# How the norm factors of the attention's outputs and of the mixers reach all partitions: two small transfers through DRAM in place of a matmul with a diagonal

## The chip, the cores and the metric

The kernel runs on one core of one Trainium2 chip. The metric is the device time of one execution in microseconds (us). Below, PE is the matmul engine, DVE the vector engine, ACT the scalar engine, POOL the GpSimd engine and SP the engine from whose queue most transfers are started; a transfer can also be started from POOL or ACT. Each engine works through its own instructions strictly in the order in which they stand. An instruction that has to wait therefore holds up everything behind it on its engine. SBUF is the on-chip memory with 128 partitions, PSUM the banks that PE writes.

## The reference

One step of a one-layer hybrid decoder. A prompt of 1024 tokens with 16 meta tokens ahead of it and 8 running sequences with 4 new tokens each go through the same layer, 1072 tokens in all. In float32:

```
u   = rmsnorm(h, norm1_g) @ w_in            # q, k, v, z, xbc, dt
ao  = sliding-window attention (window 128, sinks)          # 512 wide
y   = ssd_scan(conv(xbc), dt, ...) + xs * d_skip
so  = rmsnorm(y * silu(z), ssm_out_g)                       # 512 wide
h   = h + concat(rmsnorm(ao, attn_out_g), so) @ w_out
h   = h + relu(rmsnorm(h, norm2_g) @ w_up)**2 @ w_down
out = rmsnorm(h, norm_f_g)
```

The change touches two of these norms: that of the attention's outputs `ao` and that of the mixers' outputs `y * silu(z)`. Each needs, per token, the factor (mean of squares + 1e-6) to the power -1/2 over 512 values.

## The kernel before, in words

Activations lie transposed: features on the partitions, tokens along the free axis. The tokens are cut into 9 tiles: tile 0 holds the 32 sample tokens and the 16 meta tokens, tiles 1 to 8 hold 128 prompt tokens each. Three neighbouring tiles make a chunk, and the large matmuls work chunk by chunk (three chunks of about 384 tokens).

A float32 matmul is emulated for the projections: a matrix is split into a high and a low part of a faster float32 format, and three products are added. Such a group is 24 matmuls (12 for half the depth). Five stages follow each other: input projections with the attention of the tiles between them (to about 299 us), the output projection with the mixers of the tiles (the SSD scan, to about 411 us), the second half of the output projection with the second norm, the up projection, and the down projection with the last norm.

In the first two stages the work around the change is written as Python generators. `interleave` takes a stream of matmul groups and a list of chains with starting slots: in each slot every live chain is advanced to its next `yield`, and then the stream issues its next group. So a `yield` in a chain means "one matmul group later". `attn_block(i)` of tile i starts in the slot `START[i]`, 3.3 slots after its neighbour; `mixer(i)` starts 2.25 slots after its neighbour. This program order is a wish, not yet the order on the engines: the framework that builds the program gives each instruction its place in its engine's row by the priority that the program order gives it and by when it expects the operands to be there. So it can move an instruction ahead of others, and does.

A tile's norm goes like this. `norm_o(i)` (attention) or `gate(i)` (mixer) lets ACT square the 4x128 values of each token (`sqo`, `sqy`). `rms_bcast` then adds the four blocks, on POOL for the attention (line 369 and 370) and on DVE for the mixers, and PE multiplies them with a column of ones, so that the sum of squares of token p stands on partition p, one number per partition. `rstd_of` turns it into the factor `rsb`: one DVE instruction (line 322) and a power on POOL (line 323). The factor is needed the other way round, though: on every partition, along the free axis. ACT scales the identity matrix by the factor, which gives a diagonal matrix `dg` (line 378), and PE multiplies a matrix of ones with it. All 128 partitions of a PSUM bank (tag `pt` in the attention, `s` in the mixers) then hold the factors of the 128 tokens. DVE multiplies the tile by that bank: line 773 (`qT<-qT,pt`) in the attention, four instructions of line 1192 (`xs<-xs,vec,s`) in a mixer. From these results ACT and DVE or POOL make the split operands (`acth`, `actl`) of the output projection, and the first projection that reads them comes a stage or several groups later.

`late_of(i)` lets the attention's broadcast wait for a slot in which no other chain wants a `pt` bank.

Of the kernel before, what the change touches and what calls it, by code (L numbers as in the profile page):

```python
# [9 lines left out]
F32 = mybir.dt.float32  # L10
# [10 lines left out]
NT = 9  # L21
# [167 lines left out]
def f(ap):  # L189
    return ap.bitcast(F32)  # L190
# [3 lines left out]
def body(ctx: ExitStack, tc: tile.TileContext, xT, xm, win, wdt, wo, wu, wd, ck, cv, sc, st, sT, vec, consts,  # L194
         y, kp, vp, cv_, hp, ko, kn, vo, vn, hsm):
    nc = tc.nc
    PE, ACT, DVE, POOL, SP = nc.tensor, nc.scalar, nc.vector, nc.gpsimd, nc.sync
    vec_in, sc_in, st_in, sT_in = vec, sc, st, sT

    def pool(name, bufs=1, **kw):  # L200
        return tc.tile_pool(name=name, bufs=bufs, reuse_waits="tile", **kw)

    def mm(out, a, b, start, stop, on=False):
        PE.matmul(out, lhsT=a, rhs=b, start=start, stop=stop, skip_group_check=on)  # L204
# [3 lines left out]
    dram = ctx.enter_context(pool("dram", space=bass.MemoryType.DRAM))  # L208
# [40 lines left out]
    class Ahead:  # L249
# [9 lines left out]
        def next(self):  # L259
            while self.fns and len(self.got) <= self.n:  # L260
                self.more()
            return self.got.pop(0)
# [56 lines left out]
    def rstd_of(out, ssq, n):  # L319

        w = out.shape[-1]
        DVE.tensor_scalar(out=out, in0=ssq, scalar1=1.0 / n, scalar2=EPS, op0=ALU.mult, op1=ALU.add)
        POOL.tensor_tensor(out=out, in0=out, in1=nhalf[:out.shape[0], :w], op=ALU.pow)  # L323
# [11 lines left out]
    def act_cols(X, i):  # L335

        ch = i // 3
        a, w = TOKM[i][0] - CM[ch][0], TOKM[i][1]
        return X[ch][0][1][:, :, a:a + w], X[ch][1][1][:, :, a:a + w]
# [20 lines left out]
    pa = w2.enter_context(pool("pa"))  # L360
# [3 lines left out]
    def ps_tile(tag):  # L364
        return pps.tile([128, 512], F32, name=tag, tag=tag, bufs=1 if tag == "o" else 2)

    def rms_bcast(wk, eng, bank, sq, rows, n, *tags, late=0):

        eng.tensor_tensor(out=sq[:, 0:2], in0=sq[:, 0:2], in1=sq[:, 2:4], op=ALU.add)
        eng.tensor_tensor(out=sq[:, 0], in0=sq[:, 0], in1=sq[:, 1], op=ALU.add)  # L370
        yield
        yield
        ps = bank(*tags[:1])
        mm(ps[:rows, 256:257], sq[:, 0], ones[:, 0:1], True, True)
        rs = wk.tile([128, 1], F32, name="rsb", tag="rsb", bufs=2)
        rstd_of(rs[:rows], ps[:rows, 256:257], n)
        dg = wk.tile([128, 128], F32, name="dg", tag="dg", bufs=2)
        ACT.activation(out=dg[:rows, :rows], in_=ident[:rows, :rows], func=AF.Copy, scale=rs[:rows])
        for _ in range((2 if eng is DVE else 1) + late):
            yield  # L380
        ps = bank(*tags[1:])
        mm(ps[:, :rows], ones[:rows, :], dg[:rows, :rows], True, True)
        return ps
# [313 lines left out]
    def attn_block(i):  # L697
# [56 lines left out]
        o = po[:, :4 * rows].rearrange("p (r t) -> p r t", r=4)  # L754
        ACT.copy(out=qT[:, :, q0:q0 + rows], in_=o)
        yield from norm_o(i, o)

    START = [0] + [24 + round(3.3 * (i - 1)) for i in range(1, NT)]

    def late_of(i):  # L760

        if i == 0 or i == NT - 1:
            return 0
        taken = {START[n] + q for n in range(1, NT) for q in (3, 4)}
        return next(n for n in range(9) if START[i] + 8 + n not in taken)

    def norm_o(i, o_ps=None):
        r0, rows = TOK[i][0], TOKM[i][1]
        o = qT[:, :, r0:r0 + rows]
        sq = pa.tile([128, 4, 128], F32, name="sqo", tag="sqo", bufs=1)  # L770
        ACT.activation(out=sq[:, :, :rows], in_=o if o_ps is None else o_ps[:, :, :rows], func=AF.Square)
        ps = yield from rms_bcast(pa, POOL, ps_tile, sq[:, :, :rows], rows, 512, "o", "pt", late=late_of(i))
        DVE.tensor_tensor(out=o, in0=o, in1=ps[:, :rows].unsqueeze(1).broadcast_to([128, 4, rows]), op=ALU.mult)

    def attn_sample():
# [87 lines left out]
    def first():  # L863
        yield from attn_sample()
        kS.append(pa.tile([128, 2, 2, 2, 128], F32R, name="kS", tag="kS"))
        split_k(0)
        yield
        yield from norm_o(0)
# [44 lines left out]
    sq = {}  # L913
    w3 = ExitStack()
    sp = w3.enter_context(pool("sp"))
# [38 lines left out]
    for a, b in ((xs0, xs), (bc0, bc)):  # L954
        POOL.tensor_copy(out=a[:, :, 0:32].rearrange("p j (b t) -> p j b t", t=4),
                         in_=b[:, :, 0:56].rearrange("p j (b t) -> p j b t", t=7)[:, :, :, 0:4])
# [75 lines left out]
    def xcols(i):  # L1032
        if i == 0:
            return xs0, bc0[:, 0:2], bc0[:, 2:4]
        a = conv_col(TOK[i][0])
        return xs[:, :, a:a + 128], bc[:, 0:2, a:a + 128], bc[:, 2:4, a:a + 128]
# [4 lines left out]
    def ssd(i):  # L1041
# [70 lines left out]
        else:  # L1112
# [8 lines left out]
            for j in range(4):  # L1121
                yield
                if j == 3:
                    yield
                yield from sample_state(j, xw, Bt, eA)
        yield from gate(i)

    Bm = [None]
# [51 lines left out]
    def gate(i):  # L1180

        r0, rows = TOK[i][0], TOKM[i][1]
        y = xcols(i)[0][:, :, :rows]
        zt = sp.tile([128, 4, 128], F32, name="zt", tag="zt", bufs=2)
        SP.dma_start(out=zt[:, :, :rows], in_=zd[:, :, r0:r0 + rows])
        DVE.scalar_tensor_tensor(out=y, in0=y, scalar=0.5, in1=zt[:, :, :rows], op0=ALU.mult, op1=ALU.mult)
        sq = sp.tile([128, 4, 128], F32, name="sqy", tag="sqy", bufs=1)
        ACT.activation(out=sq[:, :, :rows], in_=y, func=AF.Square)
        yield
        ps = yield from rms_bcast(sp, DVE, ptile, sq[:, :, :rows], rows, 512)  # L1190
        for j in range(4):
            DVE.scalar_tensor_tensor(out=y[:, j], in0=y[:, j], scalar=vec[:, V_GS + j:V_GS + j + 1], in1=ps[:, :rows],
                                     op0=ALU.mult, op1=ALU.mult)
        hi, lo = act_cols(X, i)
        ACT.copy(out=hi, in_=y)
        POOL.tensor_tensor(out=lo, in0=y, in1=f(hi), op=ALU.subtract)
# [28 lines left out]
    rb = pu.tile([128, TM], F32, name="rb")  # L1225
# [6 lines left out]
    def bank(tag):  # L1232
        return pp5.tile([128, 512], F32, name=tag, tag=tag, bufs=3 if tag == "b" else 2) if tag != "g" else gps()
# [490 lines left out]
    for i, (j, k) in enumerate(down):  # L1724
# [19 lines left out]
        if j == 3 and 6 <= k < 6 + 2 * NE:  # L1744
            n, x = (k - 6) // 2, (k - 6) % 2
# [70 lines left out]
    for i, (c, k, ms) in enumerate(last):  # L1816
# [6 lines left out]
        if k == 0:  # L1823
            ps = {3: ps3} if c and ms == (3,) else {m: bank(t) for m, t in zip(ms, "ccgg" if c == 0 else "bbg")}
# [42 lines left out]
```

## Time and profile before

| | before |
|---|---|
| time, median of 3 runs | 1129.27 us (1129.19 to 1129.62) |
| the profiled execution | span 1128.1 us from the first to the last instruction; the page gives no other time of it |
| PE, share of the span busy | 98% |
| DVE | 74% |
| ACT | 50% |
| POOL | 20% |
| granted PE clock | 0.998 |

The 1128.1 us are the stretch between the first and the last instruction of one execution; the 1129.27 us are the whole of an undisturbed one, 1.2 us more. In the views below a row of a timeline reads: start in us from the span's start, length in us, engine, line of the kernel, operation, tile written, an arrow, tiles read, and in square brackets how long the engine had been idle before it and which instruction ended that. Consecutive matmuls overlap, so the time one costs is the distance from its start to the start of the next. A group of rows is written with its count, and "fp32" matmuls of the plain kind appear as two records each.

### The profile page before, as it was taken

To read this page: it belongs to the slowest core of one execution; us is meant where nothing else is said; L and a number is where in the kernel's file an instruction comes from. 1 tells how busy PE (TensorE), PEld (TensorE's weight loads), DVE (VectorE), ACT (ScalarE), POOL (GpSimd) and SP (SyncE) were. 2 spreads that over 40 slices of the span, in tenths; PEclk is the share of its full clock that TensorE was granted. 3 is DMA by queue.
4 is the path that set the end of the run, shared out by engine and by line. 5 is a ranking of instruction groups with operands and counts; after the bars stand their busy time and mean duration, and the time that the engine had idled before them with its cause. 6 is when DMAs were issued, how large, how long until landed. Compare 5 with 4: busy or idle time off the path is not lost.

```text
span 1128.1 us, 21791 instructions
## 1 busy us (share of the span) xinstructions
PE 1110.9 (98%) x8403; PEld 1072.7 (95%) x8403; DVE 838.3 (74%) x1624; ACT 569.6 (50%) x1205; POOL 223.5 (20%) x291
## 2 busy tenths in 40 slices
PE   8999999999999999999999999999999999999997
PEld 8989988889888899999999999999999999999997
DVE  6646888985788968998877777766599656867483
ACT  8312467575675748854444444444434334546361
POOL 0442365664344441210000000000000000000001
PEclk9999999999999999999999999999999999999999
DMA  8131100111466476666653443524999654465273
GB/s 287 70 98 38 38 24 34 38 53 42 144 211 196 142 268 219 211 191 216 211 190 106 162 153 134 178 90 170 384 307 322 191 172 109 118 197 169 76 229 111
DMA packets 84424, 177.64 MB, mean 157 GB/s; under 512 B 10692, under 2 KB 32740, under 8 KB 82272
## 3 DMA queue, kind: packets, MB, share of 16 engines
q1 hardware_dynamic: 77392, 141.59, 40.2%
q0 software_dynamic: 6224, 33.74, 7.5%
q8 instruction: 66, 1.08, 0.4%
q10 hardware_dynamic: 704, 0.92, 0.2%
q14 instruction: 38, 0.31, 0.1%
HBM read 125.49 MB, written 50.72 MB: 156 GB/s over the span
## 4 chain that ended last, share of the span: by engine, by line
PE 77%; DVE 10%; ACT 5%; issue 3%; DMA 3%; POOL 1%; POOLq 0%; SPq 0%; ACTq 0%; DVEq 0%
PE g L204 42%; PE b L204 19%; PE c L204 9%; PE s L204 3%; PE o L204 1%; ACT p L681 1%; DMA wraw<-in_win 1%; DVE Qs L712 1%; PE y L204 1%; DMA wdr<-in_wd 1%; DMA wraw<-in_wo 1%; DVE Sd L1612 1%; PE pt L745 1%; DVE p L679 1%; DVE bc L526 1%
## 5 line engine op out<-in xcount | busy, mean ns | idle before, releaser
L204 PE MATMUL g<-acth,whi 128*128 128x384 f32 (+2 forms) x528 | 161.9, 331 | 0.2 <-DVE qT L456 0.2
L204 PE MATMUL g<-acth,wlo 128*128 128x384 f32 (+2 forms) x528 | 159.3, 327 | 1.2 <-DVE hb L996 1.2
L204 PE MATMUL g<-actl,whi 128*128 128x384 f32 (+2 forms) x432 | 140.6, 325 | 0.0
L1625 ACT CAST ts<-tr 128x528 fp32r<-128x528 f32 x92 | 58.2, 632 | 119.2 <-PE b L204 99.2
L1626 DVE TENSOR_TENSOR ts<-tr,ts 128x528 fp32r<-128x528 f32 x92 | 64.9, 705 | 54.5 <-ACT ts L1625 53.8
L204 PEld LDWEIGHTS g<-acth,whi 128*128 128x128 f32 x528 | 97.3, 188 | 2.1 <-issue 1.0
L204 PEld LDWEIGHTS g<-acth,wlo 128*128 128x128 f32 x528 | 97.1, 188 | 1.5 <-DVE hb L996 1.3
L204 PEld LDWEIGHTS g<-actl,whi 128*128 128x128 f32 x432 | 81.4, 189 | 0.1
L323 POOL TENSOR_TENSOR rs<-rs,nhalf 128x3 f32<-128x3 f32 x9 | 10.4, 1153 | 334.5 <-DMA wdq<-in_wd 285.5
L1341 ACT COPY s<-g 128x264 f32<-128x264 f32 x90 | 33.9, 377 | 62.0 <-PE g L204 61.5
L236 POOL TENSOR_TENSOR wlo<-wraw,whi 128x256 fp32r<-128x256 f32 x56 | 50.0, 924 | 11.8 <-ACT whi L233 11.6
L1414 POOL DMA_DIRECT2D u<-u x16 | 8.5, 533 | 177.0 <-ACT u L1357 147.2
L1346 DVE TENSOR_TENSOR u<-b,s 128x264 f32<-128x264 f32 x64 | 27.4, 429 | 19.5 <-PE b L204 10.1
L735 POOL TENSOR_TENSOR p<-p,sm 128x512 f32<-128x512 f32 (+1 forms) x32 | 34.3, 1093 | 31.4 <-DVE sm L733 29.6
L1351 ACT ACTIVATE u<-u 128x528 f32<-128x528 f32 x42 | 27.1, 646 | 26.4 <-DVE u L1350 26.4
L204 PE MATMUL b<-ts,w7y 128*128 128x264 f32 x279 | 39.3, 285 | 0.0
L204 PE MATMUL g<-ts,whi 128*128 128x264 f32 x279 | 38.9, 284 | 0.0
L204 PE MATMUL g<-ts,w7y 128*128 128x264 f32 x279 | 38.9, 283 | 0.0
L204 PE MATMUL b<-ts,whi 128*128 128x264 f32 x279 | 38.9, 284 | 0.0
L204 PE MATMUL g<-ts,wlo 128*128 128x264 f32 x270 | 38.0, 285 | 0.0
L204 PE MATMUL b<-ts,wlo 128*128 128x264 f32 x270 | 37.3, 282 | 0.0
L681 ACT ACTIVATE p<-p,nm 128x257 f32<-128x257 f32 (+1 forms) x64 | 31.3, 492 | 11.0 <-DVE nm L679 10.8
(584 smaller groups left out, 3475.7 us busy)
## 6 DMA issues: line engine op xcount, KB each, us to landing
tr<-u SPq DMA_DIRECT2D x92, 264.0 KB, 3.1
wraw<-in_wu SPq DMA_DIRECT2D x38, 512.0 KB, 4.0
wdr<-in_wd SPq DMA_DIRECT2D x68, 256.0 KB, 4.0
u<-t POOLq DMA_DIRECT2D x16, 1056.0 KB, 5.6
wraw<-in_win SPq DMA_DIRECT2D x16, 512.0 KB, 3.7
u<-u POOLq DMA_DIRECT2D x10, 792.0 KB, 3.6
wraw<-in_wo SPq DMA_DIRECT2D x24, 256.0 KB, 2.9
h<-he SPq DMA_DIRECT2D x16, 264.0 KB, 5.2
```

The source lines that it names most:

```text
L204: PE.matmul(out, lhsT=a, rhs=b, start=start, stop=stop, skip_group_check=on)
L236: eng.tensor_tensor(out=lo[:, n], in0=raw[:, n], in1=f(hi[:, n]), op=ALU.subtract)
L526: DVE.scalar_tensor_tensor(out=acc, in0=cb[:, j:j + CL], scalar=cw_(j), in1=acc, op0=ALU.mult, op1=ALU.add)
L679: DVE.tensor_tensor_reduce(out=s_out[:, 0:W], in0=ps, in1=mask, scale=-scale, scalar=nsink, op0=ALU.add, op1=ALU.min, accum_out=nm)
L681: ACT.activation(out=s_out[:, 0:W + 1], in_=s_out[:, 0:W + 1], func=AF.Exp, bias=nm, scale=-1.0, accum_out=sm)
L712: DVE.tensor_tensor(out=Q[oth, g, :, :rows], in0=src, in1=f(Q[own, g, :, :rows]), op=ALU.subtract)
L735: POOL.tensor_tensor(out=p[:rows, r:r + 2, :W], in0=p[:rows, r:r + 2, :W], in1=sm[:rows, r:r + 2].unsqueeze(2).broadcast_to([rows, 2, W]), ...
L1341: ACT.copy(out=s[:, c], in_=ps[c][:, :TQ])
L1346: DVE.tensor_tensor(out=out[:, c], in0=ps[c][:, :TQ], in1=s[:, c], op=ALU.add)
L1351: ACT.activation(out=x, in_=x, func=AF.Square)
L1625: ACT.copy(out=t[:, 0], in_=x)
L1626: DVE.tensor_tensor(out=t[:, 1], in0=x, in1=f(t[:, 0]), op=ALU.subtract)
```

## The change

In the first eight tiles of each of the two norms the diagonal matrix and the matmul with it go. The column of factors `rsb` is written by a transfer from POOL's queue into a small DRAM tensor (128 numbers of 4 bytes). One slot later a transfer in SP's queue reads that tensor back as a row of 128 numbers and writes it to every partition, into an SBUF tile `rbc` of 128x128 numbers. One slot after that (and `late` more) the tile is multiplied by `rbc` as before by the PSUM bank. The last tile, number 8, of each norm keeps the old way. The tile `rbc` takes its place from the same two buffers as `dg` had.

```diff
+    rsd = {}
+
-    def rms_bcast(wk, eng, bank, sq, rows, n, *tags, late=0):
+    def rms_bcast(wk, eng, bank, sq, rows, n, *tags, late=0, key=None):
...
         rstd_of(rs[:rows], ps[:rows, 256:257], n)
+        if key:
+            rd = rsd[key] = dram.tile([128, 1], F32, name=f"rd{key}")
+            POOL.dma_start(out=rd[:rows], in_=rs[:rows])
+            yield
+            rb = wk.tile([128, 128], F32, name="rbc", tag="dg", bufs=2)
+            SP.dma_start(out=rb[:, :rows], in_=rd[:rows].rearrange("p q -> q p").broadcast_to([128, rows]))
+            for _ in range(1 + late):
+                yield
+            return rb
         dg = wk.tile([128, 128], F32, name="dg", tag="dg", bufs=2)
         ACT.activation(out=dg[:rows, :rows], in_=ident[:rows, :rows], func=AF.Copy, scale=rs[:rows])
         for _ in range((2 if eng is DVE else 1) + late):
             yield
...
-        ps = yield from rms_bcast(pa, POOL, ps_tile, sq[:, :, :rows], rows, 512, "o", "pt", late=late_of(i))
+        ps = yield from rms_bcast(pa, POOL, ps_tile, sq[:, :, :rows], rows, 512, "o", "pt", late=late_of(i), key=f"o{i}" if i < NT - 1 else None)
...
-        ps = yield from rms_bcast(sp, DVE, ptile, sq[:, :, :rows], rows, 512)
+        ps = yield from rms_bcast(sp, DVE, ptile, sq[:, :, :rows], rows, 512, key=f"y{i}" if i < NT - 1 else None)
```

PE loses 16 matmuls and ACT 16 instructions; POOL gains 16 transfers and SP 16. In the first stage the order of PE is otherwise the same. In the mixers' stage the framework also puts other instructions of all engines into a slightly different order.

Three places show what moves. The first is DVE in the attention of tile 3, eleven rows behind the one that starts the factor (`rsb`, line 322). Before, the multiply of `qT` by the bank `pt` stands behind the scaling of the next projection (`cb<-g,rb`):

```order
L694 TENSOR_TENSOR kS<-kT,kS 64x128
L695 TENSOR_TENSOR kS<-kT,kS 64x128
L733 RECIPROCAL sm<-sm 128x4
L447 TENSOR_TENSOR cb<-g,rb_133 128x384
L773 TENSOR_TENSOR qT<-qT,pt 128x4x128
L526 SCALAR_TENSOR_TENSOR bc<-cb,vec,bc 128x1096
```

With the change (its line numbers are up to 11 higher):

```order
L705 TENSOR_TENSOR kS<-kT,kS 64x128
L706 TENSOR_TENSOR kS<-kT,kS 64x128
L744 RECIPROCAL sm<-sm 128x4
L784 TENSOR_TENSOR qT<-qT,rbc 128x4x128
L458 TENSOR_TENSOR cb<-g,rb_133 128x384
L537 SCALAR_TENSOR_TENSOR bc<-cb,vec,bc 128x1096
```

The multiply stands one place earlier, ahead of `cb`, though the program order has it a slot later. In tile 4 the same happens, and in tiles 2 and 6 it moves ahead of more rows; in tiles 1, 5 and 7 its place is unchanged.

The second place is SP in the attention of tiles 1 to 5. Before, one load of weights (`wraw`) stands behind the other:

```order
L630 DMA out_kp<-kT 128x128
L631 DMA out_vp<-vt 128x128
L231 DMA wraw<-in_win 128x1024 x9
L897 DMA out_cv_<-tail 128x216
L231 DMA wraw<-in_win 128x1024
L668 DMA zd<-thz 128x304
```

With the change (`rdo` is the DRAM tensor of one tile):

```order
L231 DMA wraw<-in_win 128x1024 x2
L384 DMA rbc<-rdo_1743 128x128
L231 DMA wraw<-in_win 128x1024
L384 DMA rbc<-rdo_1939 128x128
L231 DMA wraw<-in_win 128x1024
L384 DMA rbc<-rdo_2203 128x128
L231 DMA wraw<-in_win 128x1024
L384 DMA rbc<-rdo_2413 128x128
L908 DMA out_cv_<-tail 128x216
```

A read of factors stands between every two loads of weights; each waits there until its write has landed.

The third place is DVE at the end of the mixers, with tiles 7 and 8. Before (each group of `xs<-xs,vec,s` belongs to the `rsb` above it):

```order
L1192 SCALAR_TENSOR_TENSOR xs<-xs,vec,s 128x128 x4
L322 TENSOR_SCALAR rsb<-s 128x1
L246 TENSOR_TENSOR wlo<-wraw,wlo 128x512
L971 TENSOR_TENSOR hb<-hb,g 128x288
L1192 SCALAR_TENSOR_TENSOR xs<-xs,vec,s 128x128 x2
L971 TENSOR_TENSOR hb<-hb,g 128x384
L1192 SCALAR_TENSOR_TENSOR xs<-xs,vec,s 128x128 x2
```

With the change:

```order
L322 TENSOR_SCALAR rsb<-s 128x1
L246 TENSOR_TENSOR wlo<-wraw,wlo 128x512
L982 TENSOR_TENSOR hb<-hb,g 128x288
L1203 SCALAR_TENSOR_TENSOR xs<-xs,vec,s 128x128
L1203 SCALAR_TENSOR_TENSOR xs<-xs,vec,rbc 128x128 x4
L1203 SCALAR_TENSOR_TENSOR xs<-xs,vec,s 128x128
L982 TENSOR_TENSOR hb<-hb,g 128x384
L1203 SCALAR_TENSOR_TENSOR xs<-xs,vec,s 128x128 x2
```

Tile 7's four multiplies, which stood ahead of the `rsb` of tile 8, now stand behind it, between the multiplies of tile 8.

## The prediction

> **What bounds the kernel now.** I read the page first, then the busy times of the two stages that the change touches (rows: stretch, length, busy us of each engine with its number of instructions, granted clock, DMA share and GB/s).
>
> ```profile
> span 1128.1 us, 21791 instructions
> PE 1110.9 (98%) x8403; PEld 1072.7 (95%) x8403; DVE 838.3 (74%) x1624; ACT 569.6 (50%) x1205; POOL 223.5 (20%) x291
> ...
> 125.00:300.00 175.00, 172.22 (x1108) 157.82 (x1107) 138.33 (x311) 107.26 (x277) 95.83 (x124) 1.00 0.14 41
> 300.00:330.00 30.00, 28.38 (x223) 23.83 (x222) 26.59 (x53) 22.07 (x59) 10.89 (x11) 1.00 0.76 229
> 330.00:411.00 81.00, 79.32 (x586) 70.43 (x585) 69.39 (x161) 49.49 (x123) 36.96 (x37) 1.00 0.57 175
> ```
>
> PE is busy nearly all the time in both stages, at full clock, so a matmul taken away should be worth its time. But DVE has 138.33 of 175 us and 69.39 of 81 us of work, so PE is not far ahead of it. The list of what PE waited for says where it already is not alone:
>
> ```profile
> PE pt L745 <- POOL p L735: 1.7, 4, 0.6
> ```
>
> Four times PE waited for the softmax rows that POOL scales. The chain of waits (start, length, what), followed back from the end, shows what set those moments:
>
> ```profile
> 172.16 4.18 PE g L204 x24
> 176.34 0.02 issue
> 176.36 0.49 DVE cb L447
> ...
> 211.40 0.94 ACT whi L233
> 212.34 1.22 ACT bc L524
> ...
> 230.29 0.39 POOL p L735
> ...
> 241.95 0.88 PE pt L745 x6
> ...
> 344.48 0.69 DVE hn L1099
> ...
> 354.27 1.12 DVE xs L1192 x4
> ...
> 364.23 0.29 ACT dg L378
> ...
> 367.06 0.49 PE s L204 x2
> ```
>
> From 176.36 to 241.95 us, the attention of tiles 2 to 4, the chain runs over DVE, ACT and POOL, and not over PE. From 344.48 us to the multiply at 354.27 and on to ACT at 364.23 it again does not pass PE. Elsewhere in the two stages it is PE's.
>
> **What goes from PE.** Each broadcast is two records; I take the distance from its start to the next other matmul. First and last of the seven attention tiles that go (1 to 7; tile 0 is alike), then first and last of the eight in the mixers:
>
> ```profile
> 168.76 0.38 PE L204 MATMUL pt<-dg,ones 128*128 128x128 f32 x2
> 169.08 1.51 PE L204 MATMUL o<-pT,vt 128*64 128x512 f32 x6
> ...
> 285.79 0.38 PE L204 MATMUL pt<-dg,ones 128*128 128x128 f32 x2
> 286.10 1.94 PE L204 MATMUL o<-pT,vt 128*64 128x512 f32 x8
> ...
> 340.17 0.49 PE L204 MATMUL s<-dg,ones 128*128 128x128 f32 x2
> 340.59 1.09 PE L204 MATMUL y<-Mt,xd 128*64 128x128 f32 x14
> ...
> 406.12 0.38 PE L204 MATMUL s<-dg,ones 128*128 128x128 f32 x2
> 406.34 0.28 PE L204 MATMUL s<-ones,sqy 128*128 128x1 f32 x2
> ```
>
> Attention: 8 x 0.32 = 2.57 us (tile 0 has 0.33). Mixers: 0.42 where small matmuls follow and 0.22 where large ones do; three of the first kind, three of about the second (0.24 once) and two that stand together at 0.66 make 2.60. In all 5.17 us.
>
> Not all of it is on the path. The broadcasts of attention tiles 2, 3 and 4 lie in the stretch that DVE and ACT set: 3 x 0.32 = 0.96 us only lengthen PE's waits. The same holds for the second mixer's 0.42, at 349.7 us. That leaves 5.17 - 1.38 = 3.79. ACT's own instruction (`dg`) is on the chain once, 0.29 us at 364.23; the other 15 lie beside waits of ACT. Gain: **4.08 us**.
>
> **What comes in its place.** The factor now travels: power on POOL, start of the write on POOL, landing, SP sees it and starts the read, landing, multiply on DVE. No such pair is in the trace. The nearest rows (line, queue, count, KB, median us from start to landing; the last one is POOL's time for starting a transfer):
>
> ```profile
> s1d<-s POOLq DMA_DIRECT2D x6, 264.0 KB, 3.2
> zt<-zd SPq DMA_DIRECT2D x1, 64.0 KB, 2.4
> out_kn<-kT SPq DMA_DIRECT2D x1, 16.0 KB, 1.4
> dtw<-in_wdt SPq DMA_DIRECT2D x1, 32.0 KB, 3.8
> L1368 POOL DMA_DIRECT2D s1d<-s x6 | 3.3, 542 | 12.3 <-ACT s L1341 12.3
> ```
>
> Lower bound of the pair: twice the smallest store, 2.8 us. Upper bound: the store from POOL's queue and the slowest small load, 3.2 + 3.8 = 7.0. For the write I take the middle of 1.4 (its size, another queue) and 3.2 (its queue, far larger), 2.3; for the read of 64 KB the row of that size, 2.4. Estimate: **4.7 us** from the end of the power to `rbc`.
>
> [...]
>
> Tile 3 of the attention decides the first stage, for there DVE and ACT set the time:
>
> ```profile
> 206.89 0.55 POOL L323 TENSOR_TENSOR rsb<-rsb,nhalf 128x1 f32<-128x1 f32 x1 [2.55 <-DVE rsb L322]
> 208.88 0.10 POOL L641 MEMSET cb<- 128x3 f32 x1 [1.45 <-DVE bc L533]
> ...
> 211.44 0.18 DVE L733 RECIPROCAL sm<-sm 128x4 f32<-128x4 f32 x1 [0.50 <-ACT p L681]
> 211.53 0.53 DVE L447 TENSOR_TENSOR cb<-g,rb 128x384 f32<-128x384 f32 x1
> ```
>
> The power ends at 207.44 us and the multiply is due behind the reciprocal at 211.6, so the pair has 4.2 us: DVE waits 4.7 - 4.2 = 0.5. Behind the multiply now stands `cb`, and ACT's `bc` reads that. `cb` ended at 212.06 and ACT, behind its `whi`, started `bc` at 212.34 (the chain above), 0.3 us later; now `cb` ends later by the multiply (0.68) and the wait, so ACT starts 0.4 + 0.5 = **0.9 us** later. That is on the chain. In tile 4 the same happens, but there the chain leaves DVE with POOL's row at 230.29, which depends on the reciprocal ahead of the multiply: nothing counted. Tile 2, moved the same way but with the factor long there: 0.1.
>
> POOL's start of the write, 0.54 us, falls into the 1.45 us for which POOL waits at 208.88; uncovered, 16 of them would cost 8.7 us. SP stands still at each read until the write has landed. Behind it in the first stage is a load of weights that waits longer anyway; in the mixers it is the loads and stores of `hb`, which three buffers keep ahead of DVE.
>
> Tile 5 has the tightest place, and tile 7 the tightest of the mixers:
>
> ```profile
> 245.08 0.55 POOL L323 TENSOR_TENSOR rsb<-rsb,nhalf 128x1 f32<-128x1 f32 x1 [3.19 <-DVE rsb L322]
> 247.02 0.57 DVE L447 TENSOR_TENSOR g<-g,rb 128x384 f32<-128x384 f32 x1 [0.96 <-PE g L204]
> 247.50 0.68 DVE L773 TENSOR_TENSOR qT<-qT,pt 128x512 f32<-128x512 f32 x1
> 249.89 0.48 DVE L679 CUSTOM_DVE_ANT_0 p<-s,cmk,vec 128x256 f32<-128x256 f32 x1 [1.02 <-PE s L204]
> ...
> 404.21 0.66 POOL L323 TENSOR_TENSOR rsb<-rsb,nhalf 128x1 f32<-128x1 f32 x1 [0.31 <-DVE rsb L322]
> 410.67 0.61 DVE L1192 SCALAR_TENSOR_TENSOR xs<-xs,vec,s 128x128 f32<-128x128 f32 x2 [1.73 <-PE s L204]
> ```
>
> Tile 5: power done at 245.63, multiply due at 247.50, 1.9 us, so DVE waits 2.8. Queued behind it is the scores' reduction (`p`, line 679), for which ACT, POOL and then PE wait. DVE had 0.96 + 1.02 us of idle here, and PE writes three `g` banks ahead; I count 0.2 for tiles 5 to 7. Mixer 7: power done at 404.87, so `rbc` at 409.6, and DVE gets there at 410.67 or later; but a large load stands ahead of this read in SP's queue. With mixer 0, whose multiply is also near, 0.4 for the mixers.
>
> **The sum.** 4.08 - (0.9 + 0.1 + 0.2 + 0.4) = 2.48 us gained. Against the profiled execution: span 1128.1 - 2.5 = 1125.6. The median of the runs lies 1.2 above that span, so I predict 1129.27 - 2.48 = **1126.8 us**. Its own range goes from all losses away (1125.2) to losses twice as large (1128.4).
>
> **Rivals.** (1) *The DVE row pays for the whole.* The pair takes longer than 4.7 us, and DVE, which cannot pass the multiply, holds the chain. With a pair of P, tiles 3 and 4 lose 0.4 + (P - 4.2) each, tile 5 half of what exceeds its 1.9 + 2.0 us, and mixers 0.4 to 1.2. At P = 5.3 that is 3.0 + 0.7 + 0.4 = 4.1, the whole gain; at 6.4 it is 5.2 + 1.3 + 1.1 = 7.6, so 3.5 us slower: 1132.8. For it: small loads of 3.8 us, DVE at 79% and 86%. Against it: the transfers are idle 86% of the first stage (share 0.14), and tile 4 may hide its part. [...]
>
> (2) *The new order of the mixers eats their gain.* The framework reordered that stage, and PE is idle there for only (30.00 - 28.38) + (81.00 - 79.32) = 3.3 us, so any reorder can cost. If the mixers' 2.60 us are lost, 0.1 us slower than before: 1129.4. For it: DVE is the fuller engine there. Against it: the order was made with eight matmuls fewer, and nothing long was put ahead of the scan.
>
> (3) *Everything counts.* DVE does not wait and the stretch of tiles 2 to 4 is PE's after all, since PE waits only 1.7 us there: 5.17 us, 1124.1.
>
> (4) *The change does not do what it says*: 16 matmuls stay. The order of PE shows them gone; 1129.3.
>
> **Chances and range.** Forecast 0.46, (1) 0.18, (2) 0.18, (3) 0.16, (4) 0.02. What one measurement can tell from no change is 0.2%, 2.26 us, so faster means below 1127.0. Two thirds of the forecast's range lie there: 0.31 + 0.16 = 0.47 faster. Same: 0.15 of the forecast, 0.14 of (2), (4): 0.31. Slower: (1) and 0.04 of (2): 0.22. Range for 8 in 10: from 1124.0, rival (3), to 1131.5, where (1) stands at P = 6.0.
>
> **What would show it.** Right: `pt<-dg` and `s<-dg` only once each; `rbc` landing 4 to 5.5 us after the power; DVE waiting for `rbc` about 0.5 us at tiles 3 and 4 and 2 to 3 us at tile 5; PE still busy for 98% and its waits for line 735 longer by 1 to 2 us. Wrong: a pair above 5.3 us; waits of PE for DVE in the attention of over 3 us together; in the mixers, PE idle more than 4 us longer; or a first stage that ends later than 299 us.

## The result and the profile after

The changed kernel takes **1241.74 us** (median of 4 runs, 1236.28 to 1245.51), the kernel before 1129.23 us beside it: a ratio of 1.0989, interval 1.096 to 1.1017. The prediction was 1126.8 us, in a range from 1124.0 to 1131.5. The change costs 112.5 us where a gain of 2.5 was forecast.

First the page of the changed kernel (its span, the busy time of each engine, and the granted clock in 40 slices of 31 us), then the busy times of three stretches of it in the columns of the prediction's second view:

```profile
span 1239.0 us, 21783 instructions
PE 1139.8 (92%) x8371; PEld 1095.0 (88%) x8371; DVE 840.1 (68%) x1624; ACT 565.3 (46%) x1189; POOL 235.1 (19%) x307
...
PEclk9999998878889878899999999999999999999998
```

```profile
125.00:200.00 75.00, 66.53 (x422) 61.75 (x423) 54.93 (x115) 38.85 (x96) 40.34 (x52) 0.95 0.10 30
200.00:300.00 100.00, 74.31 (x400) 64.95 (x399) 55.85 (x136) 43.97 (x116) 42.99 (x53) 0.83 0.10 30
...
420.00:517.00 97.00, 67.19 (x420) 59.82 (x418) 54.55 (x120) 32.88 (x79) 28.08 (x31) 0.84 0.49 104
```

The 32 records of the sixteen matmuls are gone (8403 to 8371), ACT has 16 instructions fewer and POOL 16 more. And PE, which was busy for 98% of the time, is busy for 92%: its idle time grew from 1128.1 - 1110.9 = 17.2 us to 1239.0 - 1139.8 = 99.2 us, by 82.0. Its busy time grew too, by 28.9 us, though it has less to do. The row of the clock shows why: between 125 and 517 us PE no longer has its full clock (0.83 from 200 to 300 us, where it was 1.00). So the 110.9 us between the two spans are 82.0 us more of idle PE and 28.9 us more of busy PE.

Two marks cut the program into the two stages that the change touches and the rest: the first `hb<-hb,g` on DVE (end of the first projection group behind the attention) and PE's first `b<-` matmul (the up projection). First the kernel before, then the changed one:

```profile
305.40 0.45 DVE L996 TENSOR_TENSOR hb<-hb,g 128x288 f32<-128x288 f32 x1 [0.98 <-DMA hb<-in_xm]
455.62 0.37 PE L204 MATMUL b<-xb11h,wlo 128*128 128x264 f32 x1
```

```profile
361.33 0.43 DVE L1007 TENSOR_TENSOR hb<-hb,g 128x288 f32<-128x288 f32 x1
563.81 0.37 PE L204 MATMUL b<-xb11h,wlo 128*128 128x264 f32 x1
```

The attention's stage ends 55.9 us later, the mixers' stretch is 202.5 us long instead of 150.2, 52.3 more, and the rest 2.7 more. (The 299 us of the prediction and of the expectations below are the attention's last multiply, at 299.24 us before; the first mark lies some 6 us behind it.)

The list of waits of the changed kernel names what stands in both stages (who waits, for what: us in total, times, longest), DVE first, then PE:

```profile
DVE qT L784 <- DMA rbc<-rdo: 63.9, 8, 9.9
DVE xs L1203 <- DMA rbc<-rdy: 44.4, 8, 10.4
```

```profile
PE s L204 <- DVE nm L690: 16.5, 3, 6.6
PE s L204 <- DVE e L1181: 10.2, 1, 10.2
PE o L204 <- POOL sqo L372: 9.9, 2, 5.1
PE pt L756 <- POOL p L746: 9.6, 8, 4.5
```

DVE, which waited for a transfer only once in these stages before (1.0 us, the row of line 996 above), stands 108.3 us in front of the sixteen multiplies. PE waits for what is queued behind them. The attention of tile 3, the place that the prediction chose, shows it row by row:

```profile
224.39 0.56 POOL L323 TENSOR_TENSOR rsb<-rsb,nhalf 128x1 f32<-128x1 f32 x1 [1.77 <-DVE rsb L322]
225.24 0.60 POOL L381 DMA_DIRECT2D rdo<-rsb  x1 [0.29 <-POOL rsb L323]
228.94 0.18 DVE L744 RECIPROCAL sm<-sm 128x4 f32<-128x4 f32 x1 [0.50 <-ACT p L692]
232.95 0.33 SPq L384 DMA_DIRECT2D rbc<-rdo  x1
237.85 0.69 DVE L784 TENSOR_TENSOR qT<-qT,rbc 128x512 f32<-128x512 f32 x1 [8.73 <-DMA rbc<-rdo]
238.46 0.55 DVE L458 TENSOR_TENSOR cb<-g,rb 128x384 f32<-128x384 f32 x1
239.05 1.30 ACT L535 ACTIVATE bc<-cb,vec 128x1096 f32<-128x1096 f32 x1 [9.20 <-DVE cb L458]
245.29 0.59 PE L204 MATMUL o<-ones,sqo 128*128 128x1 f32 x2 [5.13 <-POOL sqo L372]
```

The power ends at 224.95 us; the write leaves at 225.24 and SP can start the read at 232.95, 7.7 us later; the multiply runs at 237.85. From power to multiply it is **12.9 us**, not 4.7. DVE idles 8.73 of them. `cb` and ACT's `bc` wait behind the multiply (ACT 9.20 us), and PE, which had matmuls of the projections left, uses them up and then idles for 5.13 us in front of the next sum of squares: its squares (`sqo`) are ACT's work, queued behind `bc`. The same view of transfers as in the prediction (KB, us from issue to landing) says which leg it is:

```profile
rbc<-rdo SPq DMA_DIRECT2D x7, 64.0 KB, 4.8
rbc<-rdy SPq DMA_DIRECT2D x7, 64.0 KB, 4.2
...
rdo<-rsb POOLq DMA_DIRECT2D x7, 0.5 KB, 7.9
rdy<-rsb POOLq DMA_DIRECT2D x7, 0.5 KB, 8.4
```

The write of 512 bytes takes about 8 us. That is 1.6 times the read of 64 KB in the attention and twice that in the mixers, and longer than the 264 KB store from the same queue took before (3.2).

### The profile page after: what moved, and what is told of

It is laid out like the page before. It is cut to its first block, busy times and chain, and to the rows that moved or that the text cites. A ratio compares the mean times of both kernels' runs of the same rounds, so it can differ in the third digit from the quotient of the medians.

```text
span 1239.0 us, 21783 instructions
## 1 busy us (share of the span) xinstructions
PE 1139.8 (92%) x8371; PEld 1095.0 (88%) x8371; DVE 840.1 (68%) x1624; ACT 565.3 (46%) x1189; POOL 235.1 (19%) x307
## 4 chain that ended last, share of the span: by engine, by line
PE 49%; issue 4%; DVE 3%; DMA 2%; POOL 1%; ACT 0%; SPq 0%; POOLq 0%; ACTq 0%; DVEq 0%
PE g L204 24%; PE b L204 17%; PE c L204 8%; DMA rdy<-rsb 1%; DVE Sd L1623 1%; DVE ts L1637 0%; DMA wraw<-in_wo 0%; DVE wdr L1631 0%; DMA wdr<-in_wd 0%; POOL actl L1207 0%; DVE Sd L1622 0%; DVE wlo L1294 0%; POOL sq L988 0%; DVE whi L1294 0%; DMA hb<-hd 0%
## 5 line engine op out<-in xcount | busy, mean ns | idle before, releaser
L204 PE MATMUL g<-acth,whi 128*128 128x384 f32 (+2 forms) x528 | 170.6, 348 | 9.4 <-DVE hb L982 5.1
L204 PE MATMUL g<-acth,wlo 128*128 128x384 f32 (+2 forms) x528 | 164.2, 335 | 0.1
L204 PE MATMUL g<-actl,whi 128*128 128x384 f32 (+2 forms) x432 | 146.2, 339 | 0.0
L204 PEld LDWEIGHTS g<-acth,whi 128*128 128x128 f32 x528 | 104.4, 203 | 12.5 <-DVE hb L982 5.4
L204 PEld LDWEIGHTS g<-acth,wlo 128*128 128x128 f32 x528 | 101.1, 196 | 0.7 <-DVE hb L1007 0.2
L204 PEld LDWEIGHTS g<-actl,whi 128*128 128x128 f32 x432 | 86.4, 200 | 0.0
L236 POOL TENSOR_TENSOR wlo<-wraw,whi 128x256 fp32r<-128x256 f32 x56 | 52.0, 958 | 12.1 <-ACT whi L233 11.9
L784 DVE TENSOR_TENSOR qT<-qT,rbc 128x512 f32<-128x512 f32 (+1 forms) x8 | 5.1, 643 | 63.9 <-DMA rbc<-rdo 63.9
L204 PEld LDWEIGHTS s<-kS,Qs 128*128 128x128 f32 x144 | 21.1, 221 | 22.8 <-DVE nm L690 17.9
L1203 DVE SCALAR_TENSOR_TENSOR xs<-xs,vec,rbc 128x128 f32<-128x128 f32 (+1 forms) x32 | 9.4, 335 | 44.4 <-DMA rbc<-rdy 44.4
L204 PE MATMUL s<-kS,Qs 128*128 128x256 f32 (+2 forms) x144 | 24.2, 320 | 16.5 <-DVE nm L690 16.5
```

The costliest lines, as they stand in the source:

```text
L236: eng.tensor_tensor(out=lo[:, n], in0=raw[:, n], in1=f(hi[:, n]), op=ALU.subtract)
```

## The experiments

Ratios are against the kernel before, timed on the same chip in the same rounds.

**Each stage alone.** The key is given to one of the two norms only:

```diff
-        ps = yield from rms_bcast(sp, DVE, ptile, ..., key=f"y{i}" if i < NT - 1 else None)
+        ps = yield from rms_bcast(sp, DVE, ptile, ..., key=None)
```

> Only the attention's eight norms take the transfers; the mixers keep the diagonal. Theory A (DVE stands in front of each multiply until the pair of transfers has landed, 13 us instead of the 4.7 of the prediction, and the two stages add up): the first stage ends near 356 us as in the changed kernel and the mixers take their old 112 us, 1129 + 57 = about 1186 us (1180 to 1192). Theory B (one of the two stages carries nearly all of the loss and the other only inherits its delay): under 1150 or over 1220.

Measured: 1182.1 us, ratio 1.0468 (1.0449 to 1.0487).

> Only the mixers' eight norms take the transfers. Theory A: the first stage ends at 299 us as before, the mixers take 161 us instead of 112, about 1178 us (1170 to 1186). Theory B: under 1150, or over 1220.

Measured: 1180.1 us, ratio 1.0449 (1.0432 to 1.0466). Both lie where theory A put them. The two stages lose about alike, 53.0 and 51.0 us, and together they give 104 of the 112.5 us. Neither inherits its loss from the other.

**The transfers without a reader.** Diagonal and matmul stay as before, and write and read are made beside them:

```diff
         if key:
             rd = rsd[key] = dram.tile([128, 1], F32, name=f"rd{key}")
             POOL.dma_start(out=rd[:rows], in_=rs[:rows])
-            yield
-            ...
         dg = wk.tile([128, 128], F32, name="dg", tag="dg", bufs=2)
         ACT.activation(out=dg[:rows, :rows], ...)
-        for _ in range((2 if eng is DVE else 1) + late):
+        yield
+        if key:
+            rb = wk.tile([128, 128], F32, name="rbc", tag="dg", bufs=2)
+            SP.dma_start(out=rb[:, :rows], in_=rd[:rows]...)
+        for _ in range((1 if eng is DVE else 0) + late):
             yield
```

> All 16 pairs of transfers are made at their places, but nothing reads what they bring: diagonal, matmul and multiply stand as before. Theory A (the wait of DVE at the multiply is the cause): within 3 us of the kernel before, 1127 to 1133, with SP still standing 8 us at each read. Theory C (SP, which stands at each read until its write has landed, holds back the loads of weights, or the transfers slow others): over 1160, with PE waiting for weights.

Measured: 1164.3 us, ratio 1.032 (1.0298 to 1.0343). The first stage ends at 303.8 us, so SP's standing costs nothing that can be seen there. But the mixers lose 35 us. By its time this is theory C; but what comes late is not weights but, as the next run shows, the loads of `hb`. Two rows of its waits tell that the run does not price SP alone (SP's own queue first, then ACT):

```profile
SPq L387 <- DMA rdy<-rsb: 26.7, 4, 8.2
```

```profile
ACT dg L383 <- DMA rbc<-rdy: 26.4, 4, 8.9
```

Diagonal and unread tile shared two buffers, and ACT stood 26.4 us until a read had landed. So the read was sent elsewhere, into a DRAM tensor:

```diff
-            rb = wk.tile([128, 128], F32, name="rbc", tag="dg", bufs=2)
+            rb = dram.tile([128, 128], F32, name=f"rbc{key}")
```

> As the unread transfers, but the read goes into a DRAM tensor that nobody reads: in the run before, the diagonal of a mixer shared its two buffers with the unread tile, and ACT stood 26 us for them, so that run does not price SP's standing alone. Diagonal, matmul and multiply as before. Theory C (SP in front of the read holds back the mixers' loads and stores of hb by itself): 1140 to 1160. If the 35 us were ACT's wait for the shared buffer: 1128 to 1135.

Measured: 1159.6 us, ratio 1.0261 (1.0241 to 1.0281). ACT's wait for the tile is gone, and 30 us of loss remain. Its waits for SP and DVE:

```profile
SPq L387 <- DMA rdy<-rsb: 26.0, 4, 9.3
```

```profile
DVE hb L1005 <- DMA hb<-in_xm: 15.7, 3, 10.9
```

SP stands at a read for up to 9.3 us until its write has landed; the loads of `hb` behind it come late, and DVE waits up to 10.9 us for one. So theory C holds in the mixers: without any reader, the transfers and SP's standing at them cost 30 us, 28.7 of them in the mixers' stretch. (The first stage ends at 306.6 us here and at 303.8 in the run before, though nothing reads the transfers in either. A difference of one or two us there can come with the order alone.)

**Why is the write slow?** First its queue is changed, then its shape:

```diff
-            POOL.dma_start(out=rd[:rows], in_=rs[:rows])
+            SP.dma_start(out=rd[:rows], in_=rs[:rows])
```

> The changed kernel, with the write of the 128 factors started from SP's queue instead of POOL's. Theory Q (the 8 us of the write are the cost of POOL's queue): the write lands in 2 to 3 us, the pair falls from 13 to about 8, DVE's waits of 108 us fall to under 50, and the time to 1165 to 1195. Theory P (they are the cost of 128 pieces of 4 bytes, whatever the queue): the write still takes 7 to 8 us and the time stays within 10 us of 1242.

Measured: 1225.1 us, ratio 1.0846 (1.0831 to 1.0861). The 17 us below the changed kernel lie outside the 10 that I allowed, and where they come from was not looked for. But the write is as slow from SP's queue:

```profile
rdo<-rsb SPq DMA_DIRECT2D x7, 0.5 KB, 7.6
rdy<-rsb SPq DMA_DIRECT2D x7, 0.5 KB, 8.9
```

```diff
-            POOL.dma_start(out=rd[:rows], in_=rs[:rows])
+            with tc.issue_after(power):
+                POOL.dma_start(out=rd[:rows].rearrange("p q -> q p"), in_=sq[0:1, 0, :rows])
```

> The changed kernel, with the write from POOL's queue taking one row of 128 numbers from one partition (a row of squares, not the factors, which the output then lacks) instead of one number from each of 128 partitions. Theory P (pieces of 4 bytes): the write lands in 2 to 3 us, DVE's waits fall to under 50 us, 1165 to 1195. Theory Q (POOL's queue): the write still takes 7 to 8 us, within 10 us of 1242.

Measured: 1154.2 us, ratio 1.0212 (1.0197 to 1.0227), with

```profile
rbc<-rdo SPq DMA_DIRECT2D x7, 64.0 KB, 2.8
rbc<-rdy SPq DMA_DIRECT2D x7, 64.0 KB, 3.3
...
rdo<-sqo POOLq DMA_DIRECT2D x7, 0.5 KB, 1.6
rdy<-sqy POOLq DMA_DIRECT2D x7, 0.5 KB, 3.6
```

The same 512 bytes to the same place in DRAM, from the same queue, land in 1.6 us when they come as one row from one partition, and in 7.9 us when they come as 128 numbers from 128 partitions. Theory P holds, theory Q falls. DVE's waits shrink from 108.3 to 14.9 us, and the time lies 11 us below the range that theory P had given.

**The prediction's own conditions.** In one_row the write held the tile of squares, and the next tile's squares could wait for it. So the row is taken from the tile of ones:

```diff
+            with tc.issue_after(power):
+                POOL.dma_start(out=rd[:rows].rearrange("p q -> q p"), in_=ones[0:1, :rows])
```

> The changed kernel, with the write taking one row of 128 ones from one partition of a tile that is never written again (started behind the power on POOL; the factors are left out of the output). So the pair is as short as the prediction took it, about 4.7 us, and no tile of squares is held by the write as in one_row. If the length of the pair is the only step of the prediction that failed: 1125 to 1131. If the mixers lose in another way even with a short pair (SP standing at each read, the new order): first stage within 2 us of before, mixers 10 us or more longer, 1138 to 1155.

Measured: 1150.4 us, ratio 1.0189 (1.0174 to 1.0205). For tile 3 it is 4.5 us from the power's end (209.29) to the multiply (213.74): the pair that the prediction took. DVE then waits 0.28 us at tile 3, 0.29 at tile 4 and 3.06 at tile 5, where the prediction had 0.5, 0.5 and 2.8. It also waits 1.74 us at tile 1, where nothing was counted, 2.02 at tile 6 and 1.11 at tile 7. The time is still 20.8 us above the kernel before. So the pair was not the only wrong step. The first stage ends at 306.7 us, 1.3 later than before; the mixers' stretch is 166.3 us long, 16.1 more. There DVE still stood in front of the multiplies:

```profile
345.58 0.88 DVE L1205 SCALAR_TENSOR_TENSOR xs<-xs,vec,rbc 128x128 f32<-128x128 f32 x3 [5.35 <-DMA rbc<-rdy]
```

With the same short write and no reader:

> The same with the short write (one row of ones): the read follows after about 2 to 5 us. What SP's standing costs when the pair is as short as the prediction took it: 1128 to 1133 if SP does not matter there, and then the 20 us that ones_row lost lie in front of the multiply on DVE; 1140 or more if SP alone carries them.

Measured: 1134.5 us, ratio 1.004 (1.0027 to 1.0054), 1.5 us above the first case. With a short write the transfers and SP's standing cost 4.8 us in the whole, 4.0 of them in the mixers, against 30 with the slow one: 25 us hang on the length of the write. The other 12.1 of the mixers' 16.1 us come with the multiply that reads `rbc` and with the order that goes with it; DVE's waits for `rbc` there add up to 10.5 us.

**Holding the waiting instruction back.** The framework had put the multiplies early. An edge from the last DVE instruction that was written so far, which orders without waiting, pins each to its place in the program; the multiply is written one slot later in the attention and two in the mixers:

```diff
-            for _ in range(1 + late):
+            for _ in range((2 if eng is DVE else 1) + 1 + late):
                 yield
...
-        DVE.tensor_tensor(out=o, in0=o, ...)
+        with tc.issue_after(last_dve()):
+            DVE.tensor_tensor(out=o, in0=o, ...)
```

> The changed kernel, with each multiply held behind the DVE instruction that stands ahead of it in the program's own order, one slot later still in the attention and two in the mixers; the reads on SP stay where they are. Theory A+C (two costs: DVE in front of the multiply, and SP in front of the read, which only hurts in the mixers): the first stage ends at 299 to 302 us as before, the mixers still lose 35 us as with the unread transfers: 1160 to 1175. Theory A alone: 1126 to 1140. If holding the multiply back does nothing: over 1200.

Measured: 1163.9 us, ratio 1.0306 (1.0291 to 1.0322), as theory A+C expected. The attention's first stage ends at 303.8 us and DVE waits for no transfer there. In the mixers it waits for the loads that SP holds back, and once for `rbc`:

```profile
DVE hb L1012 <- DMA hb<-in_xm: 13.8, 6, 4.9
DVE xs L1209 <- DMA rbc<-rdy: 6.1, 1, 6.1
```

The attention alone, with the same edit there; the mixers keep their diagonal:

> Only the attention's norms take the transfers, with the multiply held back as in pin12 and one slot later. Theory A: DVE no longer waits for rbc (under 5 us in all), the first stage ends 1.4 us earlier than before, as without factors, and the whole is 1127 to 1130. If the transfers hurt the first stage in another way as well (SP's loads of weights, POOL): over 1135.

Measured: 1131.1 us, ratio 1.0008 (0.9996 to 1.0019), 1.1 above the expected band and not to be told from the kernel before. DVE waits for no `rbc`, and the first stage ends at 303.7 us, 1.7 earlier than before. So in the attention a slow pair can be hidden whole, although SP stands there as long as ever:

```profile
SPq L388 <- DMA rdo<-rsb: 70.9, 7, 15.9
```

And hiding it gains nothing that can be told from no change at the end.

**Holding SP's read back as well.** The read too is pinned, two slots behind the write in the attention and three in the mixers:

```diff
-            yield
+            for _ in range(3 if eng is DVE else 2):
+                yield
             rb = wk.tile([128, 128], F32, name="rbc", tag="dg", bufs=2)
-            SP.dma_start(out=rb[:, :rows], ...)
+            with tc.issue_after(last(sp_engine)):
+                SP.dma_start(out=rb[:, :rows], ...)
```

> All 16 pairs with their slow write, but both waits held back in the order of their engines: the read on SP two slots behind the write in the attention and three in the mixers, the multiply one slot behind the read plus one more in the attention. Theory A+C (the loss is DVE in front of the multiply and SP in front of the read): SP's waits for the write fall from 33 us in the mixers to under 10, the hb loads are on time again, DVE still waits 1 to 3 us at a mixer's multiply since one slot there is shorter than the read: 1133 to 1148. If the mixers lose by something else that comes with the transfers: over 1155.

Measured: 1178.5 us, ratio 1.0433 (1.0412 to 1.0453). This expectation was wrong by 30 us and more, and its waits say why:

```profile
DVE xs L1215 <- DMA rbc<-rdy: 29.6, 5, 7.8
DVE hb L1018 <- DMA hb<-in_xm: 7.2, 3, 4.1
```

SP now stood less, but its reads had the loads of `hb` ahead of them, which wait for their own stores: the first mixer's write left at 337.4 us and its read at 362.5, the second's at 345.5 and 378.6. The wait moved from SP back to DVE. Two places in SP's row were tried in the mixers, one slot and three behind the write; the 13 us pair costs some 30 us or more at both, and no place was found where it costs nothing.

**What there was to gain.** No diagonal, no matmul, no transfer; the multiply reads ones:

```diff
-            rd = rsd[key] = dram.tile([128, 1], F32, name=f"rd{key}")
-            ...
-            return rb
+            for _ in range((2 if eng is DVE else 1) + late):
+                yield
+            return ones
```

> Diagonal, matmul and transfers are all left out, and the multiply reads a tile of ones that was there from the start (the first eight norms of each kind are therefore left out of what is computed). This is the gain alone. The prediction's sum: 4.1 us, 1125.1. The rival in which everything counts: 5.2 us, 1124.1. A rival in which DVE and ACT set both stages: under 2 us, over 1127.2.

Measured: 1132.9 us, ratio 1.0031 (1.0019 to 1.0042): slower than before, 7.8 us above the prediction's sum. The first stage does end earlier, at 304.1 us instead of 305.4, but the mixers' stretch grows from 150.2 to 152.3 us. None of the three gains came. (The profiled execution is one of the fastest of this kernel, 1131.2 us, so these stretches show only 0.9 of the 3.7 us that its median lies above the kernel before.)

The earlier end is not all the work of the missing matmuls. The mark is an instruction that waits for a load of `hb`, and the chain of waits leads over that load, first in the kernel before, then here (start, length, what):

```profile
299.31 6.07 DMA hb<-in_xm
```

```profile
298.75 5.28 DMA hb<-in_xm
```

The load starts 0.6 us earlier, and it is 0.8 us shorter.

> As no_factor, for the attention's first eight norms alone (their factors are left out of the output); the mixers keep the diagonal and its matmul. The first stage should again end 1.3 us earlier. If that gain survives: 1127.5 to 1128.5, faster or the same. If a low granted clock behind the first stage takes it back, as in no_factor: 1129 to 1131, with a stretch of half clock near 306 us.

Measured: 1130.4 us, ratio 1.0008 (0.9998 to 1.0018); the first stage ends at 303.8 us and the mixers' stretch is 151.5 us long. The second case came: a stretch at half clock behind the first stage. Then six matmuls were added ahead of it, which only keep PE busy:

```diff
             mm(pb[:M, 256 + M * g:256 + M * g + M], B_[:, g, :], C_[:, g, :], True, True)
+        if i == 0:
+            fill = ptile("y")
+            with tc.issue_after(nc.cur_bb.bb.instructions[-1]):
+                for _ in range(6):
+                    mm(fill[:, 0:128], ones, ones, True, True)
```

> no_factor_o (the attention's factors are left out) with six more matmuls of ones by ones, which nobody reads, placed where the mixers begin and PE runs small matmuls and waits, just ahead of the stretch of half clock near 306 us. If that stretch follows from PE being too little busy just before it: full clock from 300 to 320 us, and in spite of the added work not more than 1 us slower than no_factor_o, 1128.5 to 1131. If the clock falls for another reason: the stretch at 0.5 is still there, 1131 to 1133.

Measured: 1129.4 us, ratio 0.9999 (0.9989 to 1.0009). The stretch from 305 to 310 us, in the columns of the stretches above, for no_factor_o, then for fill:

```profile
300.00:305.00 5.00, 4.47 (x31) 3.56 (x31) 4.82 (x13) 3.51 (x12) 1.06 (x2) 1.00 0.86 299
305.00:310.00 5.00, 5.00 (x25) 4.75 (x24) 4.24 (x10) 4.67 (x15) 0.62 (x1) 0.66 0.94 271
```

```profile
300.00:305.00 5.00, 5.00 (x40) 4.58 (x39) 4.66 (x12) 3.72 (x12) 1.27 (x2) 1.00 0.91 321
305.00:310.00 5.00, 4.48 (x30) 3.71 (x28) 4.52 (x11) 4.80 (x15) 0.00 (x0) 1.00 0.82 273
```

With PE kept busy (5.00 of 5 us instead of 4.47) the clock stays full, and the kernel with more matmuls is not slower than the one with fewer. This is what the expectation said, but it does not show that too little work on PE is what lowers the clock. The kernel before and mixer_only have nearly the same instructions up to this place, and PE has even less to do there. Their 3.4 us up to 306.0 (as long as the half clock lasts in no_factor, below) and the 6.8 us behind it, first for before, then for mixer_only:

```profile
302.60:306.00 3.40, 2.05 (x17) 1.38 (x15) 2.42 (x9) 2.41 (x9) 1.03 (x1) 1.00 0.76 285
306.00:312.80 6.80, 6.80 (x54) 5.81 (x55) 6.23 (x16) 6.11 (x18) 1.04 (x1) 1.00 0.87 257
```

```profile
302.60:306.00 3.40, 2.12 (x17) 1.45 (x15) 2.48 (x9) 2.54 (x10) 1.03 (x1) 1.00 0.69 260
306.00:312.80 6.80, 6.80 (x27) 6.11 (x26) 4.80 (x12) 4.82 (x16) 0.85 (x1) 0.50 0.85 263
```

PE is busy for 2.05 and 2.12 of 3.4 us, and one clock stays full while the other halves. In no_factor_o PE was busy for 2.88 of the 3.4 us ahead of its half clock. So how busy PE was in such a stretch does not tell which clock follows, and fill, which moves the matmuls behind it by a microsecond, may have kept the clock full in another way. What the half clock costs in the whole is open too: the intervals of fill and no_factor_o overlap. No version that was run is measurably faster than the kernel before.

## Why the prediction was wrong, step by step

The stretches side by side (us; "SP" is a read on SP that waits for the write, "DVE" a multiply that waits for the read, placed as in the change):

| | first stage ends | mixers' stretch | time |
|---|---|---|---|
| before | 305.4 | 150.2 | 1129.2 |
| no factor at all | 304.1 | 152.3 | 1132.9 |
| short write, SP only (unread_row) | 304.3 | 154.2 | 1134.5 |
| slow write, SP only (unread_dram) | 306.6 | 178.9 | 1159.6 |
| short write, SP and DVE (ones_row) | 306.7 | 166.3 | 1150.4 |
| slow write, multiply held back (pin12) | 303.8 | 185.2 | 1163.9 |
| slow write, SP and DVE (the change) | 361.3 | 202.5 | 1241.7 |

1. **The pair, estimated at 4.7 us: wrong, 12.9 at tile 3.** This is the step that failed first, and the largest: with the short write in its place (ones_row) about 91 of the 112.5 us are gone. The write was put between a 16 KB store and a 264 KB store, 1.4 to 3.2 us, and took 7.9. Both rows were chosen by kilobytes and by queue, and neither has the shape that was slow here, 128 numbers of 4 bytes from 128 partitions (one_row: 1.6 us for the same 512 bytes from one partition); so the "upper bound" of 7.0 was no bound. Since no row of the trace resembled the operation, the range had to be far wider. The read, 2.4, took 4.8; behind a write in one row it took 2.8 (one_row). The prediction's own sign for a failure, "a pair above 5.3 us", is what came.

2. **The DVE row pays (rival 1): the right mechanism, at the wrong size.** It had a chance of 0.18 and priced tiles 3, 4 and half of 5. With 12.9 us its formula gives 2 x (0.4 + 8.7) + 4.5 + 1.2 = 23.9 us of loss. In fact every multiply of the attention became late, 63.9 us in eight waits, since each had 2 to 8 us of room where the pair needed 13, and the attention lost 55.9 us. Attention tiles 2 to 4, where DVE already set the time, were the warning; with a wait this long it became so in every tile.

3. **"Behind it ... in the mixers it is the loads and stores of `hb`, which three buffers keep ahead of DVE": wrong.** SP's standing was put at nothing. With the transfers themselves it costs 30 us in all with the slow write (unread_dram) and 4.8 with a short one (unread_row). The prediction named the cover, and didn't say what it costs when it is gone. For the first stage the step held: in pin10a SP stands there for 70.9 us, and the stage ends no later.

4. **The mixers' 0.4 us: wrong even with the short pair.** ones_row loses 16.1 us there: 4.0 come without a reader (unread_row), 12.1 with the multiply that reads `rbc`. In the first stage the prediction's terms do better: its waits of DVE at tiles 3 to 5 came within 0.3 us once the pair was short. A gain of 1.6 and losses of 1.2 would let that stage end 0.4 us earlier, and it ends 1.3 later; the waits at tiles 1, 6 and 7 were not in the sum at their size.

5. **The gain of 4.08 us: not found in the time of any run.** The attention's part was 2.57 - 0.96 = 1.6, and without factors the first stage ends 1.3 us earlier, 1.6 in no_factor_o. That looks like a hit and is partly luck: 0.8 of it is the shorter load of `hb`, and in unread, which keeps every matmul, the stage ends 1.6 us earlier as well. Here the prediction read the chain wrongly: "elsewhere in the two stages it is PE's" overlooks that load of 6.07 us, which sets the end of the first stage. In the mixers 2.2 us and 0.29 were to come on top, and the stretch is 2.0 us longer instead, as in rival 2, in which the mixers lose their 2.6 us. Two stretches at half clock, 3.4 us each, go with it in no_factor (at 306.2 and 377.9 us; 1.7 us of PE's time each); how much the new order adds is open.

6. **The clock was in no term.** Of the 110.9 us between the spans 28.9 are added busy time of PE, 34.1 if the 5.17 us of the removed matmuls are counted: the matmuls that are left run slower. A row of the page says the same, the mean of the main group (before 331 ns):

```profile
L204 PE MATMUL g<-acth,whi 128*128 128x384 f32 (+2 forms) x528 | 170.6, 348 | 9.4 <-DVE hb L982 5.1
```

7. What was right: the sixteen matmuls go, DVE is an engine that stands, and POOL's start of a write, 0.6 us, is hidden in the attention (pin10a, with its eight writes, ends that stage at 303.7 us). "PE still busy for 98%" was not: 92%. The chance of faster was a little too high for its own range: of 1125.2 to 1128.4, 1.8 of 3.2 us lie below 1127.0, which is 56% and not two thirds.

## What to carry to other kernels

Price a transfer by its shape, not by its kilobytes alone: the same 512 bytes took 7.9 us as 128 numbers from 128 partitions and 1.6 us as one row from one. Where the trace has no transfer of that shape, the range has to be as wide as that ignorance. A wait that is put into an in-order row (DVE, or the queue that starts the transfers) holds up everything queued behind it: at tile 3 DVE stood 8.73 us in front of the multiply, and ACT stood 9.20 us for the `cb` behind it. SP's standing cost nothing that showed in the attention (70.9 us of it in pin10a) and, with the transfers, 30 us in unread_dram, where DVE waited for the loads of `hb` behind it. So look at what is queued behind, place by place. Holding the waiting instruction back hid the pair where its row had the room (pin10a, 1131.1 us); in the mixers it only moved the bill (pin12 1163.9 us, pin_sp 1178.5). And a busy share of 98% does not make every small matmul worth its time: taking 32 of 8403 records away gained nothing here.

## What the runs showed of the hardware

- The write of 128 numbers from 128 partitions into 512 neighbouring bytes of DRAM: 7.9 us from POOL's queue (the changed kernel), 7.6 from SP's (write_sp). The same bytes from one partition: 1.6 us (one_row). (Medians in the attention; in the mixers 8.4, 8.9 and 3.6.) Tile 0 has 32 numbers; its two writes landed after 3.6 us in the changed kernel. With 128 it took 7.1 to 10.0 us there until SP could start the read. The 16 KB store to `out_kn`, 128 bytes from each of 128 partitions, lands in 1.4 us, so that a write comes from 128 partitions is not enough to explain 7.9. Which property of these 128 numbers makes their write slow, the size of the pieces, their number or that they share 512 bytes, was not separated.
- The read of 64 KB is slower behind the write in pieces (4.5 to 4.8 us in the attention; 3.8 in pin_sp, where most reads start some time after the write has landed) than behind the write in one row (2.8 in one_row). Why was not tried.
- The granted clock falls to 0.50 for about 3.4 us in no_factor and no_factor_o, for 6.8 us in mixer_only (above) and for 10.2 us at one place of the changed kernel (242.3 to 252.5 us). Here are three of the half-microsecond stretches of no_factor (the last three columns are clock, DMA share and GB/s):

```profile
306.00:306.50 0.50, 0.50 (x4) 0.36 (x3) 0.50 (x1) 0.50 (x4) 0.00 (x0) 0.72 0.99 185
306.50:307.00 0.50, 0.50 (x4) 0.50 (x3) 0.44 (x2) 0.35 (x2) 0.00 (x0) 0.50 0.63 246
...
309.50:310.00 0.50, 0.50 (x4) 0.50 (x4) 0.19 (x1) 0.48 (x2) 0.24 (x1) 0.86 1.22 239
```

  The stretches from 306.5 to 309.5 us all have 0.50, so the lost clock adds up to 0.14 + 6 x 0.25 + 0.07 = 1.7 us of PE's time. The kernel before has a longer gap at the same place and keeps its full clock:

```profile
305.91 0.44 PE L204 MATMUL g<-acth,wlo 128*128 128x384 f32 x1 [1.15 <-DVE hb L996]
```

  So the idle time alone does not decide it: ahead of the drop in no_factor_o PE was idle for only 0.5 us (busy for 2.88 of 3.4). What sets the clock was not shown.
